# Two-layer hybrid decoder trunk: filter parameters issued later, and adaLN chunks shifted from GpSimd to TensorE

## The chip, the core and the metric

The kernel runs on one core of a Trainium2 chip. The metric is the device time of one execution in microseconds. Three runs of the kernel before took 1825.46, 1830.45 and 1834.98 us; the median is 1830.45 us. The execution that the profiler recorded took 1834.18 us.

## The reference

All data is float32, batch 1, 512 tokens, width 1024, two layers. Cut to what matters here:

```python
cs = silu(c)
for i in range(2):
    mod = cs @ ada_w[i] + ada_b[i]              # 1024 -> 6 * 1024
    sh1, sc1, g1, sh2, sc2, g2 = split(mod, 6)
    h = rms_norm(x, norm_mix_g[i]) * (1 + sc1) + sh1
    mix = hybrid_mixer(h, ...) if i == 0 else conformer_conv(h, ...)
    x = x + g1 * mix
    h = rms_norm(x, norm_ffn_g[i]) * (1 + sc2) + sh2
    x = x + g2 * ((silu(h @ wg) * (h @ wu)) @ wd)
return rms_norm(x, final_norm_g)
```

`hybrid_mixer` runs an SSM (Mamba-2) part and a dilated attention part on one input projection and joins them in one output projection. `conformer_conv` holds a causal depthwise convolution with 31 taps per channel.

## The kernel before

The residual stream lies transposed on the chip: `xT[k]` holds 128 channels by 512 tokens, k from 0 to 7. A matrix product splits weights and activations into a high and a low part (`slab`, lines 196 to 210: one load on the queue SP, a cast on ScalarE in two halves, a subtraction in two halves, `_h` and `_l`) and issues three matmuls per k tile (`products`, lines 212 to 226). Slab buffers come in twos (`wpool`), so a slab's load waits until the subtraction of the slab two before it is done, and its cast until the matmuls of that slab are done.

The stages follow each other: input norm, SSM in four groups (`ssm_inputs` and `ssm_group`), attention in eight pairs of heads with pieces of the output projection between them (`att_pair`, `y_chunk`, `mixed_chunk`), FFN of layer 0, conformer, FFN of layer 1, final norm. The last piece of the output projection, `mixed_chunk(3, ...)`, works in two halves of 256 tokens (names `wa_0_...` and `wa_256_...`), twelve matmuls for each 128 output channels. `residual` (line 608) adds each result to `xT` on VectorE and so frees its bank in PSUM. The norm `n1` before the FFN works in the same halves: `Stat.add` squares on ScalarE (`n_q`) and sums on GpSimd or VectorE (`n_acc`, line 263); `rstd` runs a chain of small VectorE operations (`n_v`, `n_t`, `n_y`); `spread` makes `n_d` on VectorE and `n_b` on TensorE; `finish` makes `n_g`, `n_h` (ScalarE) and `n_l` (VectorE). The first FFN products of both halves (`first_banks`, names `f_a` for gate and `f_b` for up) start with the first `n_h`.

The 6 * 1024 adaLN outputs of a layer are 48 chunks of 128 columns of `ada_w`. For layer 0, chunks 0 to 15 are made on VectorE in the first stage. Chunks 16 to 23 are made on TensorE in the SSM stage (`ada_rows`, after groups 0 and 1, four chunks at a time): eight loads of 128x512 through three buffers, eight matmuls in which `cs32` holds silu(c) in the first of 32 columns, each k going to its own 32 rows of a bank (`adar`), then a copy to SBUF (`adas`) and four small matmuls that sum the rows (`adac`). Chunks 24 to 47 are made on GpSimd in the attention stage, three per pair of heads (`ada_pool`): a load on GpSimd's own queue, a product with silu(c), three additions (`adap`), and a transpose on TensorE (`ada`, line 153) with a sum on VectorE. The chunks of layer 1 are made on VectorE during the FFN of layer 0 (`side`, four chunks per call, `adaa`).

The depthwise convolution of layer 1 needs `taps` (two loads and two transposes, `rows`), `wcol` (one memset and sixteen VectorE copies, line 921) and the filters `w4[0..3]` (four GpSimd products of 128x1024, line 930).

The order of the instructions on each engine is fixed when the program is built: a scheduler in the framework simulates the program and lists each engine's instructions by the time at which they would be ready. `tc.issue_after(x)` makes the instructions of a block on x's engine stand behind x; it holds back no other engine. At run time each engine and each DMA queue takes its instructions in that order.

Of the kernel before, what the change touches and what calls it, by code (L numbers as in the profile page):

```python
# [9 lines left out]
F32 = mybir.dt.float32  # L10
# [3 lines left out]
ALU = mybir.AluOpType  # L14
# [3 lines left out]
P = 128  # L18
# [4 lines left out]
KT = D // P  # L23
# [13 lines left out]
TB = "AABBC"  # L37
XG = 4
NEG = -1e30
LB = (383, 255, 255)  # L40
# [37 lines left out]
def trunk_kernel(ctx: ExitStack, tc, a, out, dbg=None):  # L78
    nc = tc.nc
    V, S, G, PE = nc.vector, nc.scalar, nc.gpsimd, nc.tensor  # L80
# [9 lines left out]
    def bank(tag, name, shape=(P, T)):  # L90
        return psum.tile(list(shape), F32, tag=tag, name=name)
# [52 lines left out]
    adab = [pa[:, 16:64], None]  # L144
# [19 lines left out]

    def ada_rows(pool, l, j0):

        ps = bank("C", f"adar{l}_{j0}")
        for k in range(KT):
            w = pool.tile([P, 512], F32, tag="adaw", name=f"adaw{l}_{j0}_{k}", bufs=3)
            nc.sync.dma_start(w, a["ada_w"][l][k * P:(k + 1) * P, j0 * P:j0 * P + 512])  # L170
            PE.matmul(ps[k % 4 * 32:(k % 4 + 1) * 32, :], cs32[:, k, :], w, start=k < 4, stop=k >= 4)
        rw = tmp.tile([P, 512], F32, tag="st_sq", name=f"adas{l}_{j0}")
        S.copy(rw, ps)
        pm = bank("C", f"adac{l}_{j0}", (P, 4))
        for j in range(4):
            PE.matmul(pm[:, j:j + 1], rw[:, j * P:(j + 1) * P], ones[:, 0:1], start=True, stop=True)
        V.tensor_tensor(mod[l][:, j0:j0 + 4], pm, adab[l][:, j0:j0 + 4], op=ALU.add)

# [377 lines left out]

    jobs = [(0, j) for j in range(24, 48)]

# [19 lines left out]
    for g in range(GROUPS):  # L578
        ssm_group(g, *ins)
        if g < 2:  # L580
            ada_rows(ssm, 0, 16 + 4 * g)
        if g + 1 < GROUPS:
            ins = ssm_inputs(g + 1)
# [250 lines left out]
    nrm = None  # L834
# [75 lines left out]
    dwr = a["cv_w_dw"][0].rearrange("t (k p) -> (t k) p", p=P)  # L910
    taps = const.tile([P, 31 * KT], F32, name="taps")
    rows([(dwr[0:128], 128)], "dw0", taps[:, 0:128])
    rows([(dwr[128:248], 120)], "dw1", taps[:, 128:248])

    wcol = const.tile([P, KT, 4, 8], F32, name="wcol")
    V.memset(wcol[0:32, :, :, 0], 0.0)
    taps3 = taps.rearrange("p (t k) -> p k t", k=KT)
    for sft in range(4):
        for g in range(4):
            o = wcol[sft * 32:(sft + 1) * 32, :, g, 0 if sft else 1:]  # L920
            V.tensor_copy(o, taps3[g * 32:(g + 1) * 32, :, sft - 1 if sft else 3::4])
    id4 = const.tile([P, 32], F32, name="id4")
    nc.sync.dma_start(id4, a["k_cst"][:, C_I4:C_W])
    ctx_d = ExitStack()
    pre = ctx_d.enter_context(tc.tile_pool(name="pre", bufs=1))
    w4 = {}

    def filters(k):
        w4[k] = pre.tile([P, 32, 32], F32, tag="w4", name=f"w4_{k}", bufs=4)
        G.tensor_tensor(w4[k], id4.unsqueeze(1).broadcast_to([P, 32, 32]),  # L930
                        wcol[:, k, :, :].rearrange("p g m -> p (g m)").unsqueeze(2).broadcast_to([P, 32, 32]), op=ALU.mult)

    for k in range(4):
        filters(k)
    nxt = Norm("n2", CUTS)
    with tc.tile_pool(name="ada", bufs=1) as ada:
        wides = [(1, j) for j in range(0, 48, 4)]

        def side():
            for _ in range(2 if len(wides) == 2 else 1):  # L940
                if wides:
                    l, j = wides.pop(0)
                    with tc.issue_after(nrm.tail.ins):
                        ada_wide(ada, "adacc", l, j, ada_load(ada, l, j, G, 2))

        ffn(0, nrm, g_ffn0, nxt, side)
# [185 lines left out]
```

## Time and profile before

| what | value |
|---|---|
| median of three runs | 1830.45 us (1825.46 to 1834.98) |
| profiled execution, its own time | 1834.18 us |
| its span, first to last instruction | 1832.4 us |
| PE / DVE / ACT / POOL busy | 1755.0 / 1006.2 / 740.0 / 356.2 us |
| mean granted TensorE clock | 0.985 |

PE is TensorE, PEld its weight loads, DVE VectorE, ACT ScalarE, POOL GpSimd, SP the queue of the sync engine. Idle time is what the rows put in brackets: how long the engine stood, and the instruction whose end released it. PEclk is the granted clock of TensorE: 1.00 is 2.4 GHz, 0.50 is 1.2 GHz. A row that merges several instructions ends in xN.

### The profile page before, as it was taken

The numbers are of one execution on the slowest core, as the hardware profiler recorded it, in microseconds if no ns is written. First come the engines' busy times: TensorE is split into PE (matmuls) and PEld (weight loads), VectorE is DVE, ScalarE is ACT, GpSimd is POOL, SyncE is SP. The second block draws the span as 40 slices with busy tenths as digits, with TensorE's granted clock in tenths as the row PEclk, the third lists the DMA queues.
The fourth block names the chain that finished last, engine by engine and source line by source line (L and its number), as shares of the span: only waits on it lengthen the run. The fifth ranks groups of instructions, "written<-read, shape, count | busy, mean of one in ns | idle before, by whom it ended". The sixth has DMA issues, their size and how long they took to land.

```text
span 1832.4 us, 25139 instructions
## 1 busy us (share of the span) xinstructions
PE 1755.0 (96%) x9815; PEld 1434.6 (78%) x9815; DVE 1006.2 (55%) x1946; ACT 740.0 (40%) x1475; POOL 356.2 (19%) x286
## 2 busy tenths in 40 slices
PE   5999999999999999887999999999999999999998
PEld 3777677788778787666888888897677988888887
DVE  7756658455655556648765664374216743233336
ACT  6455646455444444334421221254116633132235
POOL 0013314124543433424000000013105100000001
PEclk8999999999999999998999999999999999999999
DMA  9455544445444545334455553243632522223233
GB/s 306 122 146 159 146 124 121 121 135 154 128 138 136 142 121 159 125 104 140 163 194 194 190 196 121 81 156 88 166 103 88 161 92 93 92 92 115 72 96 133
DMA packets 234755, 247.85 MB, mean 135 GB/s; under 512 B 14586, under 2 KB 200764, under 8 KB 234637
## 3 DMA queue, kind: packets, MB, share of 16 engines
q1 hardware_dynamic: 224653, 208.51, 38.1%
q0 software_dynamic: 9984, 37.75, 6.2%
q8 instruction: 77, 1.26, 0.3%
q14 instruction: 41, 0.34, 0.1%
HBM read 228.73 MB, written 8.64 MB: 130 GB/s over the span
## 4 chain that ended last, share of the span: by engine, by line
PE 83%; DVE 6%; DMA 5%; ACT 3%; issue 1%; POOL 1%; SPq 0%; DVEq 0%; ACTq 0%
PE fd L221 4%; PE fd L222 4%; PE fd L224 4%; PE fg L222 4%; PE fg L221 4%; PE fu L222 4%; PE fu L221 4%; PE fu L224 4%; PE fg L224 4%; PE cps L977 3%; PE s L733 2%; DMA ar<-a_dram 2%; PE z L221 2%; PE z L222 2%; PE z L224 2%
## 5 line engine op out<-in xcount | busy, mean ns | idle before, releaser
L221 PE MATMUL fd<-uh,wd_h 128*128 128x512 f32 (+1 forms) x448 | 148.6, 347 | 0.9 <-DVE xT L608 0.9
L209 DVE TENSOR_TENSOR wf_l<-wf_w,wf_h 128x1024 fp32r<-128x1024 f32 x88 | 106.1, 1240 | 75.4 <-ACT wf_h L208 75.4
L222 PE MATMUL fd<-uh,wd_l 128*128 128x512 f32 (+1 forms) x448 | 147.1, 344 | 0.0
L208 ACT CAST wf_h<-wf_w 128x1024 fp32r<-128x1024 f32 x88 | 87.7, 1048 | 116.5 <-PE fd L224 71.9
L263 POOL TENSOR_TENSOR n_acc<-n_acc,n_q 128x256 f32<-128x256 f32 x32 | 29.7, 928 | 525.7 <-ACT n_q L259 525.5
L222 PE MATMUL fg<-n_h,wf_l 128*128 128x512 f32 x320 | 125.3, 392 | 1.0 <-DVE wf_l L209 1.0
L221 PE MATMUL fg<-n_h,wf_h 128*128 128x512 f32 x320 | 125.4, 392 | 0.5 <-ACT wf_h L208 0.5
L222 PE MATMUL fu<-n_h,wf_l 128*128 128x512 f32 x320 | 124.8, 390 | 0.0
L221 PE MATMUL fu<-n_h,wf_h 128*128 128x512 f32 x320 | 124.6, 389 | 0.0
L759 ACT ACTIVATE s<-s,nm 128x128 f32<-128x128 f32 x192 | 79.5, 415 | 47.1 <-DVE nm L755 41.2
L208 ACT CAST wd_h<-wd_w 128x1024 fp32r<-128x1024 f32 (+1 forms) x64 | 57.1, 940 | 101.2 <-PE fd L224 81.1
L885 DVE TENSOR_TENSOR fs<-fs,fu 128x512 f32<-128x512 f32 x40 | 27.5, 688 | 127.3 <-PE fu L224 127.3
L221 PEld LDWEIGHTS fd<-uh,wd_h 128*128 128x128 f32 x448 | 84.1, 188 | 11.9 <-DVE xT L608 1.3
L608 DVE SCALAR_TENSOR_TENSOR xT<-fd,mod,xT 128x512 f32<-128x512 f32 (+1 forms) x64 | 39.0, 615 | 98.4 <-PE fd L224 98.1
L222 PEld LDWEIGHTS fd<-uh,wd_l 128*128 128x128 f32 x448 | 84.2, 188 | 10.5
L224 PE MATMUL fd<-ul,wd_h 128*128 128x512 f32 (+1 forms) x448 | 91.9, 343 | 0.0
L209 DVE TENSOR_TENSOR wd_l<-wd_w,wd_h 128x1024 fp32r<-128x1024 f32 (+1 forms) x64 | 68.2, 1099 | 34.9 <-ACT wd_h L208 34.5
L162 DVE SCALAR_TENSOR_TENSOR adaa<-adaw,cs,adaa 128x512 f32<-128x512 f32 x112 | 84.8, 758 | 2.7
L884 ACT ACTIVATE fs<-fg 128x512 f32<-128x512 f32 x40 | 23.9, 597 | 146.7 <-PE fg L224 146.7
L186 POOL TENSOR_TENSOR adap<-adap 128x512 f32<-128x512 f32 (+2 forms) x72 | 80.9, 1124 | 5.0
L224 PEld LDWEIGHTS fd<-ul,wd_h 128*128 128x128 f32 x448 | 72.9, 188 | 10.6
L224 PE MATMUL fu<-n_l,wf_h 128*128 128x512 f32 x320 | 79.1, 389 | 0.0
(410 smaller groups left out, 4555.8 us busy)
## 6 DMA issues: line engine op xcount, KB each, us to landing
adaw<-in_ada_w POOLq DMA_DIRECT2D x24, 1024.0 KB, 5.6
wf_w<-in_ffn_w_gate SPq DMA_DIRECT2D x22, 1024.0 KB, 5.3
wf_w<-in_ffn_w_up SPq DMA_DIRECT2D x22, 1024.0 KB
wd_w<-in_ffn_w_down SPq DMA_DIRECT2D x16, 1024.0 KB, 5.1
adap<-in_ada_w POOLq DMA_DIRECT2D x24, 512.0 KB, 5.4
wd_w<-in_ffn_w_down SPq DMA_DIRECT2D x16, 768.0 KB, 4.3
wa_w<-in_hy_w_out SPq DMA_DIRECT2D x20, 512.0 KB, 5.7
adaw<-in_ada_w SPq DMA_DIRECT2D x8, 1024.0 KB, 7.8
```

The lines of the kernel that those rows point to most:

```text
L162: V.scalar_tensor_tensor(acc, ws[k // 4][:, k % 4, :], cs[:, k:k + 1], acc, op0=ALU.mult, op1=ALU.add)
L186: G.tensor_tensor(w[:, 0:n], w[:, 0:n], w[:, n:2 * n], op=ALU.add)
L208: S.copy(hi[:, s:e], raw[:, s:e])
L209: eng.tensor_tensor(lo[:, s:e], raw[:, s:e], hi[:, s:e].bitcast(F32), op=ALU.subtract)
L221: PE.matmul(ps[:, cols], hi[:, o(k):o(k) + P], xh, start=k == 0, stop=False)
L222: PE.matmul(ps[:, cols], lo[:, o(k):o(k) + P], xh, start=False, stop=False)
L224: PE.matmul(ps[:, cols], hi[:, o(k):o(k) + P], acts[k][1][:, cols], start=False, stop=k == nk - 1)
L263: (V if k >= self.n - 3 else G).tensor_tensor(self.acc, self.acc, sq, op=ALU.add)
L608: V.scalar_tensor_tensor(xT[m][:, cols], ps[:, cols], mod[l][:, go + m:go + m + 1], xT[m][:, cols], op0=ALU.mult, op1=ALU.add)
L733: marks[hp, 0] = marks[hp, 1] = PE.matmul(ps[:, o:o + 2 * wd].rearrange("p (e w) -> p e w", e=2), q, k, start=True, stop=True)
L759: S.activation(s[:, o:o + wd], s[:, o:o + wd], AF.Exp, bias=nm, accum_out=l)
L977: PE.matmul(ps[g * 32:(g + 1) * 32, :], w4[k][:, g * 8 + m, :], u4[k][:, g, t:t + w], start=m == 0, stop=m == 7)
```

## The change

Three edits. The filter parameters (`taps`, `wcol`, `w4[0..3]`) are issued from the third call of `side` on, in the FFN of layer 0, their VectorE part behind the last instruction of the norm. `ada_rows` takes three chunks at a time: two loads of 128x4x384 through one buffer of their own, each followed by four matmuls of 384 columns, and it is called four times (after group 0 twice, after groups 1 and 2 once). GpSimd makes chunks 28 to 47, twenty in place of twenty-four, three per pair of heads as before, so the last pair has none.

```diff
+ADS = (16, 19), (22,), (25,), ()
...
-    def ada_rows(pool, l, j0):
+    def ada_rows(pool, l, j0, nj):
-        ps = bank("C", f"adar{l}_{j0}")
-        for k in range(KT):
-            w = pool.tile([P, 512], F32, tag="adaw", name=f"adaw{l}_{j0}_{k}", bufs=3)
-            nc.sync.dma_start(w, a["ada_w"][l][k * P:(k + 1) * P, j0 * P:j0 * P + 512])
-            PE.matmul(ps[k % 4 * 32:(k % 4 + 1) * 32, :], cs32[:, k, :], w, start=k < 4, stop=k >= 4)
+        ps, w_ = bank("C", f"adar{l}_{j0}"), nj * P
+        for i in range(2):
+            w = pool.tile([P, 4, 384], F32, tag="adaw", name=f"adaw{l}_{j0}_{i}", bufs=1)[:, :, 0:w_]
+            nc.sync.dma_start(w, a["ada_w"][l][i * 512:(i + 1) * 512, j0 * P:j0 * P + w_].rearrange("(k p) c -> p k c", p=P))
+            for k in range(4):
+                PE.matmul(ps[k * 32:(k + 1) * 32, 0:w_], cs32[:, 4 * i + k, :], w[:, k, :], start=i == 0, stop=i == 1)
...
-    jobs = [(0, j) for j in range(24, 48)]
+    jobs = [(0, j) for j in range(28, 48)]
...
-        if g < 2:
-            ada_rows(ssm, 0, 16 + 4 * g)
+        for j in ADS[g]:
+            ada_rows(ssm, 0, j, 3)
...
+    def conv_params():
+        with tc.issue_after(nrm.tail.ins):
+            rows([(dwr[0:128], 128)], "dw0", taps[:, 0:128])
+            rows([(dwr[128:248], 120)], "dw1", taps[:, 128:248])
+            V.memset(wcol[0:32, :, :, 0], 0.0)
...
+                    V.tensor_copy(o, taps3[g * 32:(g + 1) * 32, :, sft - 1 if sft else 3::4])
+        for k in range(4):
+            filters(k)
...
                 if wides:
+                    if len(wides) == 10:
+                        conv_params()
```

On TensorE the transposes of chunks 46 and 47 (`ada`, line 153) leave the last piece of the output projection, where they stood inside `wa_0_0_...` and between `wa_0_1_2` and `wa_0_1_3`; they now stand a pair of heads earlier.

On VectorE in the second half of that piece (`wa_256_...`, its residual additions at line 608, 610 in the changed program), before the change, the sixteen copies of `wcol` stand ahead of the norm's chain for the first half, which begins with `n_0_v`:

```order
L608 SCALAR_TENSOR_TENSOR xT_218<-wa_256_0_2_0_6983,mod_121,xT_218 128x256
L921 COPY wcol<-taps 32x8x7 x4
L921 COPY wcol<-taps 32x8x8 x12
L278 TENSOR_SCALAR n_0_v<-n_0_s 128x2
L608 SCALAR_TENSOR_TENSOR xT_219<-wa_256_0_3_0_7000,mod_121,xT_219 128x256
L235 TENSOR_SCALAR n_0_t<-n_0_v 128x2
```

In the changed program the chain begins one residual addition earlier:

```order
L211 TENSOR_TENSOR wa_256_1_l<-wa_256_1_w,wa_256_1_h 128x1024
L610 SCALAR_TENSOR_TENSOR xT_217<-wa_256_0_1_0_6940,mod_121,xT_217 128x256
L280 TENSOR_SCALAR n_0_v<-n_0_s 128x2
L237 TENSOR_SCALAR n_0_t<-n_0_v 128x2
L238 TENSOR_SCALAR n_0_y<-n_0_t 128x2
L610 SCALAR_TENSOR_TENSOR xT_218<-wa_256_0_2_0_6957,mod_121,xT_218 128x256
```

The copies now stand among the additions of the third adaLN slab of layer 1, in the FFN.

On VectorE at the end of the same chain, before the change (`n_0_d` feeds the broadcast `n_0_b`, `n_g` is its product, `wf_0_0_l` here is the low part of the first up slab):

```order
L238 TENSOR_TENSOR n_0_t<-n_0_y 128x2
L239 SCALAR_TENSOR_TENSOR n_0_t<-n_0_t,n_0_v 128x2
L608 SCALAR_TENSOR_TENSOR xT_223<-wa_256_1_3_0_7077,mod_121,xT_223 128x256
L240 SCALAR_TENSOR_TENSOR n_0_y<-n_0_t,n_0_y 128x2
L285 TENSOR_SCALAR n_0_d<-cst,n_0_y 128x128 x2
L209 TENSOR_TENSOR wf_0_0_l<-wf_0_0_w,wf_0_0_h 128x1024 x2
L321 TENSOR_TENSOR n_g_0_7206<-n_g_0_7206,n_0_b 128x256
```

In the changed program:

```order
L610 SCALAR_TENSOR_TENSOR xT_221<-wa_256_1_1_0_7017,mod_121,xT_221 128x256
L287 TENSOR_SCALAR n_0_d<-cst,n_0_y 128x128 x2
L610 SCALAR_TENSOR_TENSOR xT_222<-wa_256_1_2_0_7034,mod_121,xT_222 128x256
L265 TENSOR_TENSOR n_256_acc<-n_256_acc,n_256_q_7031 128x256
L265 TENSOR_TENSOR n_256_acc<-n_256_acc,n_256_q_7048 128x256
L610 SCALAR_TENSOR_TENSOR xT_223<-wa_256_1_3_0_7051,mod_121,xT_223 128x256
L323 TENSOR_TENSOR n_g_0_7145<-n_g_0_7145,n_0_b 128x256
```

`n_0_d` stands two residual additions earlier, and the subtraction of the up slab has moved behind the first four `n_g`.

On the queue SP in SSM group 0, before the change (`ar` and `ef` are the group's decay rows, `wz` and `wbc` slabs of the input projection):

```order
L505 DMA ar_0_1449<-a_dram 128x8x128
L170 DMA adaw_16_3_1070<-in_ada_w 128x512
L170 DMA adaw_16_4_1073<-in_ada_w 128x512
L170 DMA adaw_16_5_1076<-in_ada_w 128x512
L505 DMA ar_1_1491<-a_dram 128x8x128
L170 DMA adaw_16_6_1079<-in_ada_w 128x512
L200 DMA wz_1_w<-in_hy_w_in 128x8x256
```

In the changed program:

```order
L507 DMA ar_0_1456<-a_dram 128x8x128
L171 DMA adaw_16_1_1067<-in_ada_w 128x4x384
L507 DMA ar_1_1498<-a_dram 128x8x128
L202 DMA wz_1_w<-in_hy_w_in 128x8x256
L171 DMA adaw_19_0_1081<-in_ada_w 128x4x384
L557 DMA yd_dram<-y_0_846 128x4x512
L202 DMA wbc_w<-in_hy_w_in 128x8x128 x2
L171 DMA adaw_19_1_1087<-in_ada_w 128x4x384
```

Each load of a half slab stands in the queue at its place, behind it the loads of `ar`, `wz`, `wbc` and `wx`.

## Rows read from the trace of the kernel before

**Rows 1.** The page of the profile, its part 1 (busy us, share of the span, instructions per engine) and the engine line of its part 4 (the chain that ended last).

```profile
PE 1755.0 (96%) x9815; PEld 1434.6 (78%) x9815; DVE 1006.2 (55%) x1946; ACT 740.0 (40%) x1475; POOL 356.2 (19%) x286
...
PE 83%; DVE 6%; DMA 5%; ACT 3%; issue 1%; POOL 1%; SPq 0%; DVEq 0%; ACTq 0%
```

**Rows 2.** The waits of TensorE over the whole span: line waited for, total us, times, longest us.

```profile
PE ada L153 <- POOL adap L186: 8.6, 2, 6.1
...
PE n_b L288 <- DVE n_d L285: 4.7, 2, 4.0
...
PE f_a L221 <- ACT n_h L322: 4.1, 2, 3.4
```

**Rows 3.** Stretches between the end of the mixer and the first FFN: length, busy us of PE, PEld, DVE, ACT and POOL with their instruction counts, PEclk (granted TensorE clock as a share of full speed), DMA share, GB/s.

```profile
817.00:821.00 4.00, 3.63 (x15) 3.18 (x16) 1.93 (x5) 0.67 (x3) 0.92 (x1) 0.50 0.50 163
...
821.00:828.40 7.40, 7.40 (x60) 7.06 (x59) 4.29 (x5) 4.61 (x9) 5.78 (x4) 1.00 0.07 23
...
828.40:831.00 2.60, 0.09 (x2) 0.05 (x1) 0.92 (x3) 0.83 (x2) 2.60 (x5) 1.00 0.42 97
...
851.00:856.00 5.00, 1.14 (x6) 1.06 (x6) 4.96 (x5) 2.15 (x3) 5.00 (x3) 0.92 0.36 122
...
861.50:865.00 3.50, 3.44 (x16) 3.44 (x17) 3.50 (x14) 3.50 (x10) 0.00 (x0) 0.50 1.02 404
```

**Rows 4.** TensorE in order of time over the same stretches: start us, us, instruction, and in brackets the idle time before it and what ended it.

```profile
816.95 0.47 PE L153 MATMUL ada<-cst,adap 128*128 128x128 f32 x1 [6.09 <-POOL adap L186]
...
822.32 0.29 PE L221 MATMUL wa<-yh,wa_h 128*128 128x256 f32 x1
...
823.76 0.29 PE L221 MATMUL wa<-yh,wa_h 128*128 128x256 f32 x1
...
830.95 0.33 PE L153 MATMUL ada<-cst,adap 128*128 128x128 f32 x1 [2.51 <-POOL adap L186]
...
861.56 0.58 PE L221 MATMUL f_a<-n_h,wf_h 128*128 128x256 f32 x1 [3.43 <-ACT n_h L322]
...
886.81 0.60 PE L153 MATMUL ada<-cst,adaa 128*128 128x128 f32 x4
```

**Rows 5.** VectorE in order of time over the same stretches, columns as in rows 4.

```profile
809.74 2.35 DVE L209 TENSOR_TENSOR wa_l<-wa_w,wa_h 128x1024 fp32r<-128x1024 f32 x2
...
814.27 1.29 DVE L821 TENSOR_TENSOR at<-o,at 128x512 f32<-128x512 f32 x2 [2.17 <-DMA at<-w_dram]
...
839.29 4.31 DVE L921 COPY wcol<-taps 32x56 f32<-32x56 f32 x16
...
851.35 1.48 DVE L240 SCALAR_TENSOR_TENSOR n_y<-n_t,n_y 128x2 f32<-128x2 f32 x1
...
852.87 3.76 DVE L285 TENSOR_SCALAR n_d<-cst,n_y 128x128 f32<-128x128 f32 x2
...
856.55 4.08 DVE L209 TENSOR_TENSOR wf_l<-wf_w,wf_h 128x1024 fp32r<-128x1024 f32 x2
```

**Rows 6.** GpSimd in order of time (the four filter products), and the row of the tile n_d over the whole span (ns min/median/max).

```profile
850.89 7.53 POOL L930 TENSOR_TENSOR w<-id,wcol 128x1024 f32<-128x1024 f32 x4 [2.23 <-DVE n_t L238]
...
L285 DVE TENSOR_SCALAR n_d<-cst,n_y x12: 280/286/1944, 852.9 to 1459.2; 128x128 f32<-128x128 f32 x12
```

**Rows 7.** ScalarE in order of time, columns as in rows 4.

```profile
816.61 0.62 ACT L826 CAST ath<-at 128x512 fp32r<-128x512 f32 x1 [6.20 <-DVE at L823]
...
850.84 1.99 ACT L208 CAST wf_h<-wf_w 128x1024 fp32r<-128x1024 f32 x2 [0.53 <-PE wa L224]
...
861.00 1.71 ACT L322 ACTIVATE n_h<-n_g,mod 128x256 fp32r<-128x256 f32 x4 [7.85 <-DVE n_g L321]
```

**Rows 8.** The loads of the tile at over the whole span, from issue to landing.

```profile
DMA to landing us min/median/max: 4.0/4.4/6.1
```

**Rows 9.** TensorE in the SSM stage (each pair of a weight load and a matmul counts two in xN), and the transposes of the chunks from GpSimd, ns min/median/max.

```profile
127.91 1.06 PE L171 MATMUL adar<-adaw,cs 128*32 128x512 f32 x6
...
145.41 1.05 PE L171 MATMUL adar<-adaw,cs 128*32 128x512 f32 x2
...
158.09 0.95 PE L176 MATMUL adac<-ones,adas 128*128 128x1 f32 x8
...
L153 PE MATMUL ada<-cst,adap x24: 270/273/475, 420.5 to 831.0; 128*128 128x128 f32 x24
```

**Rows 10.** The queue SP and TensorE in the SSM stage, and two rows of the page's part 6 (KB of one load, median us from issue to landing).

```profile
128.98 1.31 SPq L170 DMA_DIRECT2D adaw<-in_ada_w  x3
...
136.67 1.06 PE L171 MATMUL adar<-adaw,cs 128*32 128x512 f32 x6
...
wd_w<-in_ffn_w_down SPq DMA_DIRECT2D x16, 768.0 KB, 4.3
...
adaw<-in_ada_w SPq DMA_DIRECT2D x8, 1024.0 KB, 7.8
```

**Rows 11.** VectorE in the first FFN's first stretch, and two pieces of the chain that ended last there (start us, us, what).

```profile
914.95 4.68 DVE L162 SCALAR_TENSOR_TENSOR adaa<-adaw,cs,adaa 128x512 f32<-128x512 f32 x6
...
921.18 0.69 DVE L885 TENSOR_TENSOR fs<-fs,fu 128x512 f32<-128x512 f32 x1 [1.55 <-PE fu L224]
...
902.45 1.81 PE fg L224 x8
...
907.89 1.82 PE fu L224 x8
```

More of the change, by code (lines that the diff above doesn't have):

```diff
@@ L163, in ada_wide @@
         return ada_finish(l, acc, j0, 4)
-    def ada_rows(pool, l, j0):
-        ps = bank("C", f"adar{l}_{j0}")
-        for k in range(KT):
-            w = pool.tile([P, 512], F32, tag="adaw", name=f"adaw{l}_{j0}_{k}", bufs=3)
-            nc.sync.dma_start(w, a["ada_w"][l][k * P:(k + 1) * P, j0 * P:j0 * P + 512])
-            PE.matmul(ps[k % 4 * 32:(k % 4 + 1) * 32, :], cs32[:, k, :], w, start=k < 4, stop=k >= 4)
-        rw = tmp.tile([P, 512], F32, tag="st_sq", name=f"adas{l}_{j0}")
-        S.copy(rw, ps)
+    def ada_rows(pool, l, j0, nj):
[5 more added lines that the diff above has]
+                PE.matmul(ps[k * 32:(k + 1) * 32, 0:w_], cs32[:, 4 * i + k, :], w[:, k, :], start=i == 0, stop=i == 1)
+        rw = tmp.tile([P, 512], F32, tag="st_sq", name=f"adas{l}_{j0}")[:, 0:w_]
+        S.copy(rw, ps[:, 0:w_])
         pm = bank("C", f"adac{l}_{j0}", (P, 4))
-        for j in range(4):
+        for j in range(nj):
             PE.matmul(pm[:, j:j + 1], rw[:, j * P:(j + 1) * P], ones[:, 0:1], start=True, stop=True)
-        V.tensor_tensor(mod[l][:, j0:j0 + 4], pm, adab[l][:, j0:j0 + 4], op=ALU.add)
+        V.tensor_tensor(mod[l][:, j0:j0 + nj], pm[:, 0:nj], adab[l][:, j0:j0 + nj], op=ALU.add)
     def ada_pool(pool, bufs, l, j):
@@ L910, in trunk_kernel @@
     dwr = a["cv_w_dw"][0].rearrange("t (k p) -> (t k) p", p=P)
[L911 to L921, printed above, removed]
     id4 = const.tile([P, 32], F32, name="id4")
@@ L926, in trunk_kernel @@
     w4 = {}
+    taps = const.tile([P, 31 * KT], F32, name="taps")
+    wcol = const.tile([P, KT, 4, 8], F32, name="wcol")
+    def conv_params():
[3 more added lines that the diff above has]
+            V.memset(wcol[0:32, :, :, 0], 0.0)
+            taps3 = taps.rearrange("p (t k) -> p k t", k=KT)
+            for sft in range(4):
+                for g in range(4):
+                    o = wcol[sft * 32:(sft + 1) * 32, :, g, 0 if sft else 1:]
+                    V.tensor_copy(o, taps3[g * 32:(g + 1) * 32, :, sft - 1 if sft else 3::4])
+        for k in range(4):
+            filters(k)
     def filters(k):
@@ L931, in filters @@
                         wcol[:, k, :, :].rearrange("p g m -> p (g m)").unsqueeze(2).broadcast_to([P, 32, 32]), op=ALU.mult)
-    for k in range(4):
-        filters(k)
     nxt = Norm("n2", CUTS)
```

## Prediction

> **What bounds the kernel now.** I read the page first: TensorE is busy for 1755.0 of 1832.4 us and makes 83% of the chain that ended last [rows 1]. So the time is TensorE's work plus its idle time and its slow stretches, and an edit pays only where TensorE stands or runs slow. I read TensorE's waits next: the longest wait in the list is for a transpose of adaLN chunks from GpSimd, 8.6 us in two waits, and the norm that follows adds 4.7 us (for n_d) and 4.1 us (for n_h, most of it at the first FFN) [rows 2]. Nearly all of this lies between 810 and 862 us. Then I read that stretch in the windows and in order of time. TensorE is nearly empty from 851 to 861.5 and its granted clock drops after a long idle: 0.50 (1.2 GHz) from 817 to 821 after 6.09 us of idle, 0.50 again from 861.5 to 865 [rows 3, 4]. That is the place that the first edit and the last chunks touch; the rest of the SSM and attention stages is TensorE at work.
>
> **The change part by part.** The sum is made on the profiled execution, 1834.18 us: span 1832.4 and 1.8 around it. It lies 3.7 us above the median of 1830.45, so the saving found here is taken off the median at the end.
>
> The first wait for a chunk, 6.09 us up to 816.95 [rows 4], I cost at nothing. The matmul behind it needs ath, and ScalarE makes ath from 816.61 to 817.23 [rows 7], after VectorE waited for the tile at until 814.27 [rows 5]. So ath takes the place of the chunk. The load of at may land some 1.7 us sooner without the chunk's load beside it (4.4 median against 6.1 at most [rows 8]; I take the most to be this one), but VectorE now does the 2.35 us subtraction, which it did while waiting [rows 5], between the two steps of at. Bounds: 2 us gained, 1 us lost; I take 0.
>
> The second wait, 2.51 us up to 830.95 [rows 4], goes: the matmuls behind it (wa_0_1_3) use the same slab as those ahead of it. TensorE thus goes on at 828.44 with nine pieces of twelve matmuls, one of the first half and eight of the second. A piece takes 1.44 us at full clock (822.32 to 823.76 [rows 4], clock 1.00 [rows 3]), nine take 13.0, so 841.4. VectorE still puts two subtractions (2.35 us [rows 5]) between residual additions that free banks, for which I add 1.6: 843.0.
>
> The norm's chain beside it. Before, the sixteen wcol copies held VectorE for 4.31 us ahead of it, and then the four filter products ran on GpSimd for 7.53 us [rows 5, 6]. While they ran, the two n_d took 3.76 us, and the same operation has a median of 0.286; the two subtractions took 4.08 against 2.35 without them [rows 5, 6]. Those two rows alone lost 3.2 + 1.7 us on the path from the last residual addition to n_g, and n_y beside them took 1.48. All that is gone. In the new order n_d is done before the last piece of the projection ends, so at 843.0 what is left is ScalarE's two casts of the up slab, which wait for that piece's buffer (1.99 [rows 7]) and hide n_b and n_g, then one square, and the first n_h, 0.43 (a quarter of 1.71 [rows 7]); the square has the same size, so I give it 0.43 too. That is 2.9 us. I get the first f_a at 846.0, where it was 861.56 [rows 4]: 15.5 us. The block from f_a to 886.81 [rows 4] keeps its 25.25 us, slow clock included, since a 3 us idle still stands ahead of it. Bounds of this term: 7 (n_h held to 854 by ScalarE or the up slab) and 19 (no late banks, no slow clock).
>
> The Trainium skill bears on the filters (SBUF — State Buffer, "The single rule"): the port pair that VectorE and GpSimd share is an exclusive lock, and the loser waits out the whole instruction. The trace agrees: the longest n_d took 1.94 us, one filter product 1.88 [rows 6]. The rule says that the loss moves with the filters to wherever VectorE has work.
>
> It does move, into the FFN. There VectorE gets 4.31 us of copies, and beside the four filters it loses the 4.9 us seen in the two rows above: 9.2 us, between the additions of the third slab (4.68 us for six [rows 11]) and the next fs, which frees the bank of an up product. Its cover is the 1.55 us for which VectorE waited there [rows 11], and the 5.4 us of the product that comes between (902.45 to 907.89 [rows 11]): 7.0. Left over: 2.2 us of idle TensorE. Below, 0; above, all of 4.31 + 7.53 - 7.0 = 4.8. I take 2. By the lock rule at its worst, four products each waited out in full, it is that upper end.
>
> TensorE in the SSM stage: three adar matmuls of 512 columns span 1.06 us and one alone spans 1.05 [rows 9], so those that go to different rows of the bank run beside each other and the group counts. Before there were two slabs of four groups, 8.4 us; now there are eight groups of four, 384 columns wide: 0.79 us each by columns, 1.4 if the fourth costs a third more, so 6.3 to 11.2; I take the lower half, 7.5, nearest to the rows: 0.9 gained. The adac sums grow from 8 to 12, 0.24 each (0.95 for four [rows 9]): 1.0 lost. Four transposes of 0.27 [rows 9] leave the attention stage: at most 1.1, I take 0.5. Together 0.4 gained, from 3 lost to 3 gained, which also holds what the slightly new order of groups 1 to 3 may shift. The bytes of adaLN weights are the same.
>
> The new buffer: each half slab is loaded only when the four matmuls of the half before are done, and the next loads of SP stand behind it. Before, three loads of 256 KB, the same 768 KB, were issued at 128.98 and used at 136.67 without a wait [rows 10]: 7.7 us of cover, and the new second half stands at the same place. A 768 KB load lands in 4.3 us in one row, a 1024 KB one in 7.8 [rows 10]. I take no wait; bounds 0 and 4 us in all.
>
> Sum: 15.5 - 2 + 0.4 = 13.9, so 1820.3 on the profiled execution and 1816.5 on the median.
>
> **The rivals.** First: the filters cost the FFN more than I think, a backlog that also delays the low parts of the next slabs, 9 us or so (copies and contention uncovered). Gain 15.9 - 9 = 7: 1823.5. For it: the contention seen at the norm. Against: VectorE has idle time in every period there.
>
> Second: n_h stays late. The up slab is loaded by SP only after a subtraction of the projection, cast after its last piece, and ScalarE puts this cast ahead of n_h. If f_a starts at 853 the gain is 8.6 - 1.6 = 7: 1823.5. For it: before, the cast ran at 850.84, as soon as the buffer was free [rows 7]; against: that was before the wait of n_h began.
>
> Third, slower: the single buffer. If each second half lands in 14 us in place of 7.7, because SP stands at an earlier wait or ar loads share the engines, TensorE loses 6 us in each of the four slabs, 25 in all, and the slabs of wx and wz behind come late too: 1841. It decides from a landing of about 13.5 us on. Against it: the 7.8 us of the slowest row like it [rows 10]. The Trainium skill (Trainium Kernel Development and Optimization, "Best Practices") speaks for it: it asks for double buffers so that loads run beside the work. The trace of before shows three buffers and no wait, and no row of it shows one.
>
> Fourth: the change does what it says at the norm, but the wait moves on to the first slabs of the FFN, whose loads now collide with layer 1's adaLN loads on GpSimd's queue: gain 4, 1826.5.
>
> **How the numbers follow.** Forecast 0.66, with its own range of 1810 to 1822; filters in the FFN 0.12; late n_h 0.11; collision of loads 0.06; single buffer 0.05. The measurement can tell about 0.5%, 9.2 us, from no change: faster means below 1821.3. The forecast's upper edge lies just beyond that, so faster gets 0.66 (0.64 of the forecast and 0.02 of the others), within 0.5% gets 0.29, slower 0.05. The range of 1809 to 1827 leaves out the single buffer and the best ends of the terms together.
>
> **What would show it.** Right: no wait of TensorE for GpSimd's chunks; no n_d above 0.3 us before the FFN; some 17.5 us between the end of wa_0_1_2 and the first f_a, in place of 33; a wait of about 2 us in the third FFN period at an up product; adar groups of 0.8 to 1.0 us. Wrong: a wait of TensorE at adar for a load; f_a waiting on ScalarE or on the up slab at 850 or later; an idle TensorE of 5 us or more where the filters now run; a granted clock of 0.5 in the SSM stage.

## The result, and the profile after

| | before | after |
|---|---|---|
| median | 1830.45 us | 1820.54 us (seven runs, 1814.79 to 1822.05) |
| ratio | | 0.9939, 95% interval 0.9922 to 0.9957 |
| profiled execution, its own time | 1834.18 us | 1821.43 us |
| its span | 1832.4 us | 1819.7 us |

The ratio is 11.2 us of 1830.45. The forecast was 1816.5 on the median and 1820.3 on the profiled execution. From here on "the changed kernel" is this one, and its lines stand two below those of before (one in the adaLN helpers).

The page, parts 1 and 4, as in [rows 1]:

```profile
PE 1748.2 (96%) x9851; PEld 1429.8 (79%) x9851; DVE 996.0 (55%) x1940; ACT 740.0 (41%) x1477; POOL 332.3 (18%) x266
...
PE 80%; DMA 6%; DVE 5%; ACT 3%; SPq 2%; issue 2%; POOL 1%; DVEq 0%; ACTq 0%; POOLq 0%
```

TensorE's waits, as in [rows 2] (total us, times, longest):

```profile
PE ada L154 <- DVE adaa L163: 10.1, 4, 6.6
...
PE wa L223 <- ACT ath L828: 5.0, 1, 5.0
PE adar L173 <- DMA adaw<-in_ada_w: 3.4, 1, 3.4
...
PE n_s L272 <- ACT n_q L261: 1.6, 1, 1.6
...
PE ada L154 <- DMA adaw<-in_ada_w: 0.7, 1, 0.7
PE f_a L223 <- ACT n_h L324: 0.6, 1, 0.6
...
PE ada L154 <- POOL adap L188: 0.4, 1, 0.4
```

The 8.6 us for chunks from GpSimd are 0.4, and n_d is no longer waited for. In their place stand ath (the rounded attention output, 5.0) and, new, a half slab in the SSM stage (3.4). TensorE in order of time at the places of [rows 4], at the first products of the second FFN slab pair (`fg` gate, `fu` up), and at its third pair:

```profile
815.68 0.58 PE L223 MATMUL wa<-ath,wa_h 128*128 128x256 f32 x1 [4.99 <-ACT ath L828]
...
844.49 0.61 PE L272 MATMUL n_s<-ones,n_q 128*128 128x1 f32 x4 [1.59 <-ACT n_q L261]
844.96 0.36 PE L223 MATMUL f_a<-n_h,wf_h 128*128 128x256 f32 x1
...
869.64 0.49 PE L223 MATMUL fg<-n_h,wf_h 128*128 128x512 f32 x1 [0.54 <-ACT wf_h L210]
870.87 0.66 PE L154 MATMUL ada<-cst,adaa 128*128 128x128 f32 x4 [0.73 <-DMA adaw<-in_ada_w]
...
912.48 0.44 PE L154 MATMUL ada<-cst,adaa 128*128 128x128 f32 x2 [1.82 <-DVE adaa L163]
913.08 0.50 PE L223 MATMUL fu<-n_h,wf_h 128*128 128x512 f32 x1 [0.16 <-DVE fs L887]
```

The first f_a starts at 844.96 in place of 861.56. The windows, columns as in [rows 3]:

```profile
815.60:819.60 4.00, 3.56 (x15) 3.27 (x16) 1.57 (x3) 0.68 (x3) 0.00 (x0) 0.50 0.71 261
...
845.00:848.00 3.00, 3.00 (x26) 3.00 (x27) 3.00 (x9) 2.35 (x7) 0.00 (x0) 1.00 1.01 396
```

After the wait for ath the granted clock is 0.50, as in [rows 3] after the wait for a chunk; but the first f_a now run at 1.00, where they ran at 0.50. VectorE and GpSimd around the norm and in the FFN, as in [rows 5, 6]:

```profile
840.27 0.54 DVE L287 TENSOR_SCALAR n_d<-cst,n_y 128x128 f32<-128x128 f32 x2
...
900.88 3.80 DVE L931 COPY wcol<-taps 32x56 f32<-32x56 f32 x16
904.71 7.71 DVE L163 SCALAR_TENSOR_TENSOR adaa<-adaw,cs,adaa 128x512 f32<-128x512 f32 x4
```
```profile
904.77 9.44 POOL L937 TENSOR_TENSOR w<-id,wcol 128x1024 f32<-128x1024 f32 x4 [2.76 <-DVE wcol L931]
```

The two n_d take 0.54 us in place of 3.76. The four products now meet VectorE at 904.8: four additions that take 3.1 us by [rows 11] (4.68 for six) take 7.71, and TensorE waits 1.82 + 0.16 us behind them.

### The profile page after: what moved, and what is told of

It reads as the page before. It is cut to its first block, busy times and chain, and to the rows that moved or that the text cites. A ratio compares the mean times of both kernels' runs of the same rounds, so it can differ in the third digit from the quotient of the medians.

```text
span 1819.7 us, 25180 instructions
## 1 busy us (share of the span) xinstructions
PE 1748.2 (96%) x9851; PEld 1429.8 (79%) x9851; DVE 996.0 (55%) x1940; ACT 740.0 (41%) x1477; POOL 332.3 (18%) x266
## 4 chain that ended last, share of the span: by engine, by line
PE 80%; DMA 6%; DVE 5%; ACT 3%; SPq 2%; issue 2%; POOL 1%; DVEq 0%; ACTq 0%; POOLq 0%
PE fd L223 4%; PE fd L224 4%; PE fd L226 4%; PE fu L223 4%; PE fg L224 4%; PE fu L224 4%; PE fu L226 4%; PE fg L226 4%; PE fg L223 4%; PE s L735 2%; SPq L976 2%; DMA ar<-a_dram 2%; PE cps L984 2%; PE z L223 2%; PE z L224 2%
## 5 line engine op out<-in xcount | busy, mean ns | idle before, releaser
L163 DVE SCALAR_TENSOR_TENSOR adaa<-adaw,cs,adaa 128x512 f32<-128x512 f32 x112 | 89.5, 800 | 2.5
L226 PE MATMUL fg<-n_l,wf_h 128*128 128x512 f32 x320 | 79.0, 389 | 0.0
```

Of the source, the lines that this page charges most:

```text
L163: V.scalar_tensor_tensor(acc, ws[k // 4][:, k % 4, :], cs[:, k:k + 1], acc, op0=ALU.mult, op1=ALU.add)
L226: PE.matmul(ps[:, cols], hi[:, o(k):o(k) + P], acts[k][1][:, cols], start=False, stop=k == nk - 1)
```

## The experiments

For every run the start of the same matmul was set against the first profile of before. The table splits the difference (us, less is earlier) at four of them: the start of the last projection piece (808.2 in before), the first f_a (861.6), the first fg (887.2) and the first fd (the down product, 954.4). "End" is the difference at the first fo (the transposes behind the final norm, 1793.0). Each column from "to f_a" to "to fd" is the change within its own stretch; "on the starts" below means read in this way.

| kernel | ratio to before | up to 808 | to f_a | to fg | to fd | end |
|---|---|---|---|---|---|---|
| before_again | one run | -0.9 | +0.1 | +0.1 | 0.0 | -0.8 |
| changed kernel | 0.9939 | -0.1 | -16.5 | -0.9 | +4.2 | -12.7 |
| after_again | 0.9938 | -3.2 | -17.1 | -0.9 | +4.2 | -16.8 |
| filters_only | 0.9962 | +1.6 | -12.1 | +0.2 | +5.2 | -5.2 |
| chunks_only | 0.9986 | -1.7 | -13.3 | +6.4 | +0.9 | -7.7 |
| copies_early | 0.9998 | +1.7 | -14.0 | +8.1 | +0.9 | -3.0 |
| quarters | 0.9953 | +3.4 | -16.4 | -0.9 | +4.1 | -8.0 |
| three_slabs | 0.9924 | 0.0 | -16.6 | -0.9 | +4.2 | -12.9 |
| spread | 0.9905 | -6.9 | -16.5 | -0.9 | +1.7 | -22.1 |
| spread_again | 0.9915 | -1.6 | -16.8 | -0.9 | +1.7 | -17.1 |
| spread_three | 0.9920 | +0.5 | -16.6 | -0.9 | +1.8 | -15.5 |
| spread_skip | 0.9928 | -6.1 | -15.5 | +0.4 | +1.4 | -19.7 |
| four_a_pair | 1.0084 | +26.9 | -15.2 | -1.2 | +5.1 | +16.1 |

Intervals of the ratios are 0.0014 to 0.002 to either side and stand with each run below.

### How far one profile can be trusted

**before_again**, no edit.

> The kernel before, unchanged, for a second profile: how far the start of the same matmul lies from one execution to the next. Theory (the differences of 1 to 5 us between 130 and 780 us from kernel to kernel are mostly of one execution, since the kernel with the filter edit alone has the order of before there and still shows them): differences of 1 to 4 us there against the first profile of before, under 1 us in the stretch from 810 to 960 us taken by itself. Rival (they are the kernels' own): under 1 us everywhere.

The same program differed from itself by 2.4 us at 158 us, 2.8 at 378 and 3.3 at 645, by 0.1 at 778 and 0.9 at 808; from 808 to the first fd by 0.2 in all. The theory holds. **after_again**, no edit:

> The changed kernel once more, beside the next three on the same chip. Theory: 10 to 12 us less than before (ratio 0.9935 to 0.995). Its second profile shows which of the differences up to 800 us belong to the kernel: TensorE's wait for a half slab (3.4 us in the first profile) is there again, the stalls at the first fg (about 1.3 us) and in the third period (2.0 us) are the same within 0.1 us.

1819.59 us, 0.9938 (0.9923 to 0.9953). The half slab was waited for again (3.6 us), the stalls in the FFN were 0.54, 0.72 and 1.82 us; up to 808 it was 3.1 us ahead of the first profile, from 808 to the first fd 0.6. The theory holds. So what follows rests on the last three stretches of the table; of the first one a single profile says little.

### Each edit alone

**filters_only**: in the kernel before, only the filters' edit.

```diff
+    def conv_params():
...
+                    if len(wides) == 10:
+                        conv_params()
```

> The kernel before with the filter edit alone: filter parameters behind the norm, adaLN slabs and the 24 GpSimd chunks as before. Theory (the two edits act one after the other on TensorE, and the filters hold the norm): the waits for chunks stay, about 6 and 2.5 us, the norm is as in the changed kernel; first f_a about 12.5 us earlier than before, the stalls of the first FFN periods (some 1.5 and 2.5 us) appear as in the changed kernel; 9 us less than before, ratio 0.995. Rival A (the chunks decide, the filters only fill a wait that TensorE has anyway): 3 us less or nothing. Rival B (the filter edit is the whole gain, the second chunk wait would be hidden): 11.5 us less or more, first f_a 15 us earlier.

1825.03 us, 0.9962 (0.9945 to 0.9980): 7.0 us less. The waits for chunks were 6.26 and 1.26 us, the first f_a came 12.1 us earlier counted from 808. The theory holds: its 9 us lie inside the interval (3.7 to 10.1 us), both rivals outside. From 808 to the first fd the profile gains 6.7. What is missing has two places, both of the clock. The stall of the third period is the same 1.82 + 0.16 us, but here the granted clock fell behind it, in the changed kernel it did not (fu after the stall, first filters_only, then the changed kernel, columns as in [rows 3]):

```profile
919.60:923.20 3.60, 3.48 (x9) 2.70 (x10) 2.52 (x4) 3.00 (x4) 1.98 (x2) 0.54 0.25 39
```
```profile
913.00:916.60 3.60, 3.52 (x15) 2.92 (x16) 2.52 (x4) 3.01 (x4) 1.94 (x2) 1.00 0.25 39
```

Nine matmuls in 3.6 us against fifteen. And the first f_a ran at 0.61 (851 to 854 us) behind the same wait of 1.59 us behind which they run at 1.00 in the changed kernel; the stretch from f_a to fg is 1.1 us longer (+0.2 against -0.9).

**chunks_only**: the changed kernel with taps, wcol and filters where they stood before.

```diff
+    for k in range(4):
+        filters(k)
...
-                    if len(wides) == 10:
-                        conv_params()
```

> The changed kernel with the filter parameters in their old place: four slabs of three chunks, twenty chunks on GpSimd. The scheduler here puts the sixteen copies into the attention output at the end of the last pair (between at and its low part) and the four filter products behind GpSimd's last sum of the norm. Theory: the copies cost TensorE about 3 us there, the second chunk wait (2.5 us) is gone, n_d is done before the filters begin (no n_d above 0.8 us), but the products meet n_g, n_l and the low part of the up slab, each 1.5 to 2 times as long, some 4 to 5 us ahead of or within the first FFN block; no stall at the third FFN period: 6 us less than before in all (3 to 8). Rival A (only n_d suffers from the filters): 11 us less. Rival B (whatever uses GpSimd beside the norm costs as much as before): 0 to 2 us less.

1827.47 us, 0.9986 (0.9970 to 1.0003): 2.6 us less, and no difference is not excluded. From 808 to the first f_a it gains 13.3 us. Then the four products meet the norm's VectorE work: the low part of the up slab takes 4.12 us in place of 2.35, the first n_l 2.13 in place of 0.48, and TensorE waits 3.44 us for n_h behind them. VectorE, GpSimd and TensorE in order of time:

```profile
845.48 4.12 DVE L211 TENSOR_TENSOR wf_l<-wf_w,wf_h 128x1024 fp32r<-128x1024 f32 x2
849.52 2.13 DVE L325 SCALAR_TENSOR_TENSOR n_l<-n_g,mod,n_h 128x256 fp32r<-128x256 f32 x1
```
```profile
843.75 9.67 POOL L932 TENSOR_TENSOR w<-id,wcol 128x1024 f32<-128x1024 f32 x4 [1.64 <-DVE n_acc L265]
```
```profile
855.53 0.58 PE L223 MATMUL f_a<-n_h,wf_h 128*128 128x256 f32 x1 [3.44 <-ACT n_h L324]
```

From f_a to fg that is 7.3 us more than in the changed kernel (+6.4 against -0.9), where 4 to 5 were expected; the copies cost 1.0 us, not 3. Rival A falls: the two n_d took 0.55 us and the loss came all the same. By the time, the forecast of 6 us lies just outside the interval (-0.5 to 5.5 us) and rival B's 0 to 2 us inside: the place was forecast rightly, the loss there was sized too low.

**copies_early**: copies at their old place in the program, products in the FFN (so it was meant).

```diff
+    rows([(dwr[0:128], 128)], "dw0", taps[:, 0:128])
...
+            V.tensor_copy(o, taps3[g * 32:(g + 1) * 32, :, sft - 1 if sft else 3::4])
...
```

> The changed kernel with the two loads, the transposes and the sixteen copies of the filter parameters back at their old place in the program (the scheduler puts the copies between at and its low part) and only the four filter products in the FFN. Theory (the stall of the third FFN period is the sum of copies and contention): the copies cost about 3 us in the projection, the FFN stall falls from 2.0 to under 0.5 us: 1 us slower than the changed kernel, 11.5 us less than before. Rival (the stall is contention with the products alone): it stays at 1.5 to 2 us, 3 us slower than the changed kernel.

1829.60 us, 0.9998 (0.9984 to 1.0012): the whole gain is gone. The experiment did not do what it was made for. Nothing but the late copies had held the products in the FFN; with the copies early, GpSimd ran them as soon as the first adaLN loads were issued, at 848.15, beside the low part of the up slab. The rows of VectorE, GpSimd and TensorE, and the durations of that operation around it (ns min/median/max):

```profile
848.10 9.78 DVE L211 TENSOR_TENSOR wf_l<-wf_w,wf_h 128x1024 fp32r<-128x1024 f32 x2
```
```profile
848.15 7.51 POOL L936 TENSOR_TENSOR w<-id,wcol 128x1024 f32<-128x1024 f32 x4
```
```profile
856.81 0.80 PE L224 MATMUL f_b<-n_h,wf_l 128*128 128x256 f32 x2 [5.92 <-DVE wf_l L211]
```
```profile
L211 DVE TENSOR_TENSOR wf_l<-wf_w,wf_h x4: 1211/1218/8648, 840.9 to 856.7; 128x1024 fp32r<-128x1024 f32 x4
```

One subtraction of 1.22 us took 8.65: it stood until all four products (7.51) were through. Of the FFN this run shows a third period without copies and without products: there is no stall.

### What the stall in the FFN is made of

**spread**: one product behind the loads of each of four slabs.

```diff
-        for k in range(4):
-            filters(k)
...
+                        ws = ada_load(ada, l, j, G, 2)
+                    if 6 <= len(wides) <= 9:
+                        with tc.issue_after(marks['ada'].ins):
+                            filters(9 - len(wides))
...
```

> The changed kernel with the four filter products apart: the copies where they are, then one product behind the loads of each of four slabs of layer 1, in place of four in a row. Theory (VectorE stands still for as long as a run of GpSimd products lasts: in the changed kernel four additions of the third slab took 7.71 us beside the 9.44 us of products, in place of some 3.1): each product alone costs VectorE at most about 1.9 us, inside the 1.3 to 1.5 us plus 4.9 us for which it waits in every period, so the stall of 2.0 us at the third period's up product falls under 0.5 us: 2 us less than the changed kernel, 13 us less than before. Rival (the copies of 3.8 us make the stall): it stays at 1.5 to 2 us.

1816.69 us, 0.9905 (0.9885 to 0.9925). The copies stand where they stood and TensorE waits nowhere in the period. VectorE, then GpSimd:

```profile
894.07 3.81 DVE L931 COPY wcol<-taps 32x56 f32<-32x56 f32 x16
897.91 4.65 DVE L163 SCALAR_TENSOR_TENSOR adaa<-adaw,cs,adaa 128x512 f32<-128x512 f32 x4
```
```profile
897.96 2.47 POOL L934 TENSOR_TENSOR w<-id,wcol 128x1024 f32<-128x1024 f32 x1 [2.76 <-DVE wcol L931]
...
904.05 1.93 POOL L934 TENSOR_TENSOR w<-id,wcol 128x1024 f32<-128x1024 f32 x1
```

The same four additions take 4.65 us, 3.1 less than beside four products. By the stall the theory holds and the rival falls: the copies alone fit into the cover. The ratio is lower than forecast (17.4 us less than before, forecast 13); 6.9 us of the profile's difference lie ahead of 808. **spread_again**, the same kernel beside the changed one on one chip:

> The kernel with the four filter products apart once more, on the same chip as the changed kernel. Theory (what the spreading gives is the stall of the third period and nothing else): 2 to 3 us less than the changed kernel run beside it, 13 to 14 less than before. Rival (it also shortens the attention stage, as its first profile, 3 us ahead at 748 us where the changed kernel is 4.3 behind, suggests): 6 us less than the changed kernel.

1815.67 us, 0.9915 (0.9900 to 0.9931), where after_again had 0.9938: 3.9 us between the medians, with intervals that overlap. Between fg and fd both profiles are 2.4 us better than both of the changed kernel. The 3 us that the first profile was ahead in the attention stage were not there again (2.9 behind at 748 us), so the theory is nearer. The runs with spread products have the lowest ratios of all (0.9905 to 0.9928, with three_slabs at 0.9924 among them); their intervals overlap.

**spread_skip**: in that kernel, the first call of side makes no slab.

```diff
...
+            calls.append(0)
+            for _ in range(0 if len(calls) == 1 else 2 if len(calls) > 9 else 1):
...
```

> The kernel with spread filter products, and no adaLN slab of layer 1 at the first call of side: the twelve slabs start at the second call, two each in the last two calls. Theory (the 1.3 us that TensorE waits at the first fg, for wf_h and for the first slab's transposes, come from the first slab and its load): these waits go, 1.3 us less than the kernel with spread products. Rival (they come from the first gate and up slabs of the FFN, which land late because the norm ends earlier): the wait for wf_h stays, no change.

1815.80 us, 0.9928 (0.9909 to 0.9946): no gain. The wait for wf_h at the first fg (0.54 us) and the next one (0.73) stayed. But the experiment did not do what it was made for either: the slab of the second call took the place of the first. Its additions begin on VectorE 7.5 us ahead of the first fg in both kernels (first the changed kernel, fg at 869.64, then spread_skip, fg at 865.97):

```profile
862.14 0.48 DVE L161 TENSOR_SCALAR adaa<-adaw,cs 128x512 f32<-128x512 f32 x1
```
```profile
858.46 0.48 DVE L161 TENSOR_SCALAR adaa<-adaw,cs 128x512 f32<-128x512 f32 x1
```

So neither theory nor rival is decided by it. What did change is the clock: behind the wait of 1.59 us ahead of f_a it was granted at 0.50, where spread and the changed kernel have 1.00, and the stretch to fg is 1.3 us longer than there (columns as in [rows 3]):

```profile
840.00:843.20 3.20, 3.20 (x16) 3.20 (x17) 3.20 (x10) 2.55 (x7) 0.00 (x0) 0.50 1.02 396
```

### The slabs in the SSM stage

**quarters**: the same space as two buffers.

```diff
-        for i in range(2):
-            w = pool.tile([P, 4, 384], F32, tag="adaw", name=f"adaw{l}_{j0}_{i}", bufs=1)[:, :, 0:w_]
+        for i in range(4):
+            w = pool.tile([P, 2, 384], F32, tag="adaw", name=f"adaw{l}_{j0}_{i}", bufs=2)[:, :, 0:w_]
...
```

> The changed kernel with each slab of three chunks loaded in four quarters of 128x2x384 through two buffers (the same space as one buffer of 128x4x384). Theory (the wait of 3.4 us of TensorE at the third slab is the single buffer: its second half was issued only when the first half's matmuls were done): a quarter is half as long, so the wait falls to 0 to 2 us and the SSM stage ends 1.5 to 3 us earlier than in the changed kernel. Rival (the load is late because of SP's order and the loads beside it): the wait stays at 3 us or more, no change of time.

1821.35 us, 0.9953 (0.9937 to 0.9969). TensorE's wait for these loads fell from 3.4 us to 0.9, as the theory had it, yet up to 808 us nothing was gained. The rows show why: where the changed kernel waits for the half slab, TensorE now waits for `sx`, work of ScalarE on an SSM input, and before it waited there for `sc`, such work on VectorE (first before, then quarters):

```profile
216.65 0.57 PE L221 MATMUL x<-n_h,wx_h 128*128 128x512 f32 x1 [2.45 <-DVE sc L460]
```
```profile
220.28 0.77 PE L223 MATMUL x<-n_h,wx_h 128*128 128x512 f32 x1 [3.85 <-ACT sx L459]
```

**three_slabs**: chunks 16 to 27 in the old form.

```diff
-ADS = (16, 19), (22,), (25,), ()
+ADS = (16,), (20,), (24,), ()
...
```

> The changed kernel with the old form of the adaLN slabs in the SSM stage, three of four chunks (chunks 16 to 27, after groups 0, 1 and 2), each of eight loads of 128x512 through three buffers; the same twenty chunks on GpSimd. Theory (the slabs of three chunks through one buffer cost the SSM stage 2 to 4 us: by the medians so far the kernels with them lose that much against what the end of the mixer and the FFN gain): no wait of TensorE for these loads, SSM stage 2 to 4 us shorter than in the changed kernel: 13 to 15 us less than before. Rival (the number of slabs or the moved order costs it, not the form): same time as the changed kernel within 1.5 us.

1821.17 us, 0.9924 (0.9907 to 0.9941), 2.7 us under the changed kernel by the ratio, with intervals that overlap. TensorE's wait for a load was 0.4 us in all (adar, whole span); for sc it stood 2.85 us at the same place, and at 808 the profile was where that of the changed kernel was. Neither theory nor rival is excluded by the time. **spread_three**: this form with spread products.

> The kernel with spread filter products and the three slabs of four chunks through three buffers. Theory (the wait for a half slab is taken up by later waits of the attention stage, so the form of the slabs is worth nothing at the end): within 1.5 us of the kernel with spread products run beside it. Rival (it costs its 3.4 us): 3 us less.

1815.13 us, 0.9920 (0.9904 to 0.9935), 0.5 us from spread_again: the theory holds. This wait of 3 us in the SSM stage does not show at the end within what the runs can tell.

### GpSimd free at the end, by another way

**four_a_pair**: filters_only with the 24 chunks in the first six pairs.

```diff
-        ada_some(att, 1, 3)
+        ada_some(att, 1, 4)
```

> The kernel before with the filter edit, and its 24 chunks on GpSimd made four per pair of heads in the first six pairs (in place of three in each of eight); slabs in the SSM stage as before. Theory (what the chunk edit gives at the end of the mixer comes from GpSimd's being free in the last pair, not from the twelve chunks on TensorE): no wait for a chunk there, the SSM stage as before, first f_a as in the changed kernel; 13 us less than before, against some 7 for the filter edit alone. Rival (a fourth chunk per pair overloads GpSimd, whose chunks then hold the transposes of the pairs 0 to 5): waits of TensorE for chunks of 5 us or more in the attention stage, 7 us less than before or fewer.

1849.72 us, 1.0084 (1.0066 to 1.0102), the only kernel slower than before. The end of the mixer came as hoped (15.2 us gained from 808 to f_a), but 26.9 us were lost ahead of it. Not for chunks: TensorE's waits for these are 2.4 us in all. In the changed order at stands ahead of score work on VectorE and waits for its load, and the scores of TensorE stand behind it, 5.47 us here and 6.1 once more; these two are 11.5 of the 26.9 us, the rest was not taken apart. So the theory on the end of the mixer holds, and the way to it costs more than it gives. VectorE, then TensorE:

```profile
481.58 1.29 DVE L821 TENSOR_TENSOR at<-o,at 128x512 f32<-128x512 f32 x2 [5.47 <-DMA at<-w_dram]
```
```profile
482.32 2.08 PE L733 MATMUL s<-kz,q 128*128 128x256 f32 x4 [5.47 <-DVE at L821]
```

## Why the prediction was right, step by step

The forecast of 1816.5 lay 4.0 us under the median, and 1820.3 lay 1.1 us under the profiled execution. The gain is where it was expected, at the norm, and there the forecast holds to 0.3 us. That the whole sum lands so near the profile is in part luck: 1.1 us at the first wait and 0.9 from f_a to the first fg were gained beyond it, 2.2 between fg and fd lost beyond it, and up to 808 us two profiles of the same changed kernel lie 3.1 us apart.

**The first wait costs nothing**: right. ath took the chunk's place, 4.99 us for 6.09, and in every run with the chunk edit it stood there with 4.6 to 5.0. The 1.1 us gained lie inside the bounds. As worked out, at came sooner (VectorE takes it at 810.82 in place of 814.27) and the subtraction of 2.35 us stands between its two steps. The 6.1 us that the prediction took for this load belongs to another one, issued at 566.34; the landing of this one is not in the trace.

**The second wait, the pieces and the norm, 15.5 us**: right. From the matmul behind the first wait to the first f_a the forecast had 29.05 us (816.95 to 846.0), the profile has 29.28 (815.68 to 844.96), before it was 44.61 [rows 4]. The projection's last matmul ended at 842.09, where 843.0 was forecast; the matmuls of n_b and n_s follow to 842.90, then the wait of 1.59. What the prediction did not name is the clock's part: before, the granted clock was 0.50 from 831.3 to 834.7, behind the second wait, and from 844.9 to 848.3; in the changed kernel it is 1.00 from 819.8 on. The pieces were costed at full clock, and so the sum has this gain in it. The causes have been separated: without the filters' edit the norm's stretch loses 7.3 to 9.0 us from f_a to fg (chunks_only, copies_early), without the chunk edit 4.4 less is gained up to f_a (filters_only). Neither edit gives the result alone: 7.0 and 2.6 us, 11.2 together.

**The block of f_a keeps its length, slow clock included**: wrong, by 1.1 us (24.14, from 844.96 to 869.10, in place of 25.25). TensorE stood 1.59 us ahead of it, not 3, and the granted clock stayed at 1.00. The one does not settle the other: behind the same 1.59 us the clock was low in filters_only, chunks_only, copies_early and spread_skip (0.61, 0.68, 0.50 and 0.50 in the first 3 us of f_a). With 0.54 us of idle at its end the start of fg came 0.9 us nearer to f_a.

**The filters in the FFN, 2 us, bounds 0 and 4.8**: right in place and size. The period's stall is 1.82 + 0.16 us at an up product, 2.5 us on the starts. Four products in a row are its cause, since four apart do away with it while the copies stay. The working had copies and contention as one sum of 9.2 us; here they are 3.80 and 4.6 (7.71 less 3.1), 8.4.

**What was not in the sum**: 1.3 us of idle at the first fg (0.54 and 0.73). It is in every kernel that has both edits in full; the other four with one of them or a part have 1.0 us there, for wf_l. The fourth rival spoke of a wait at this place, at 9.9 us (13.9 less the 4 it left) and for loads. The rows show another cause. The four casts of wf_h stand on ScalarE right behind the second `fs<-f_a`, which needs the last matmul of f_a; the loads of wf_w had been issued 28 and 22 us earlier (839.98 and 846.28), and others of them land in 8.5 us at most. Before, 19 matmuls of f_b came behind that last f_a (884.53 to 886.97) and covered the first cast; now 10 do (867.75 to 869.10). ScalarE before, then in the changed kernel:

```profile
884.73 0.60 ACT L884 ACTIVATE fs<-f_a 128x512 f32<-128x512 f32 x1 [0.51 <-PE f_a L224]
885.23 3.88 ACT L208 CAST wf_h<-wf_w 128x1024 fp32r<-128x1024 f32 x4
```
```profile
868.06 0.59 ACT L886 ACTIVATE fs<-f_a 128x512 f32<-128x512 f32 x1
868.55 3.88 ACT L210 CAST wf_h<-wf_w 128x1024 fp32r<-128x1024 f32 x4
```

The 0.73 us are the last addition of the first adaLN slab: VectorE makes it from 870.07 to 870.82, the transposes start at 870.87. The view names a load there, but in the other profiles with this wait it names the addition. On the starts the stretch to fd lost 4.2 in place of 2; 0.7 of this are transposes that stood ahead of fg before and now stand behind it.

**The SSM stage, 0.4 gained, bounds 3 to either side, and 0 to 4 for the buffer**: the parts are as worked out, the sum is open. An adar group takes 0.85 us (0.94 was taken), three adac sums 0.72 to 0.83. The second half of the third slab was issued when the first half's matmuls (210.41) were done, and landed 10.2 us later, where 7.8 was the slowest row like it; loads of wz (1 MB) and ar (0.5 MB) had been issued 1.1 and 0.6 us ahead of it. SP, TensorE, and the page's part 6:

```profile
211.72 1.49 SPq L171 DMA_DIRECT2D adaw<-in_ada_w  x1
```
```profile
221.94 1.02 PE L173 MATMUL adar<-adaw,cs 128*32 128x384 f32 x8 [3.36 <-DMA adaw<-in_ada_w]
```
```profile
adaw<-in_ada_w SPq DMA_DIRECT2D x8, 768.0 KB, 10.2
```

So the third rival's mechanism was there once, short of the 13.5 us from which it decides, and no wait was the wrong value to take. The Trainium skill's "Best Practices" (Trainium Kernel Development and Optimization) ask for double buffers; the trace agrees in so far as two smaller buffers cut the wait to 0.9 us, and the runs add that the time did not follow, since another wait stood at the same place (2.45 us before, 3.85 in quarters). By the ratio the changed kernel gains 11.2 us, from 808 on its profiles show 12.6 to 13.6; the 2 us between could be this stage, but two profiles have it at -0.1 and -3.2 up to 808, and no run here settles it. All profiles together say a little more. At the first matmul of the attention output (o, 399.6 in before) the ten with the chunk edit stand 2.2 to 7.6 us behind the first profile of before, 5.0 on average; the four without it 0 to 3.1, 1.9 on average. So the SSM stage seems to have lost some 3 us in place of gaining 0.4, three_slabs and spread_three (5.8 and 5.0) no less than the others, and by 808 this is made up. Why is open.

**The other rivals**: filters at 9 us in the FFN did not come, though beside the norm they do cost 7 to 9. n_h was not late: f_a at 844.96, not 853.

**The signs**: the signs of being right came, if not all to the letter: 0.4 us of waits for GpSimd's chunks, n_d at 0.35 us at most, 18.0 us between the end of wa_0_1_2 (826.98) and the first f_a. Of the signs of being wrong two came all the same: the wait at adar (3.4 us), and a granted clock of 0.50 in the SSM stage (140.6 to 144.0, 222.5 to 225.9 and 297.6 to 301.0). The second was a poor sign, since it is in before too (216.9 to 220.3).

## What to carry to other kernels

Look at what runs on GpSimd beside a chain on which TensorE waits, and move it as single instructions, each into a period in which VectorE has slack; four in a row cost TensorE 2.5 us in the FFN and 7 to 9 beside the norm, four apart in the FFN nothing that shows. Before a wait is taken away, look at what stands behind it: here the wait for a load only hid another of about the same length. When two things hold the same stretch, take each away alone as well as both: here each by itself gave 2.6 and 7.0 us, both 11.2, which the intervals do not tell from the sum. Before a difference of a few microseconds between two profiles is explained, profile the same program twice and use only the stretches in which it agrees with itself.

## What was not expected of the hardware

One VectorE subtraction was shut out for four GpSimd products in a row (8.65 us, usually 1.22, copies_early). In the changed kernel the two took turns: no addition took over 2.29 us (ns min/median/max of the tile), and the four products took 9.44 us in place of 7.51. It is not the operation that decides: in chunks_only the same two subtractions met the same products and took turns, 1.26 and 2.93 us. Nor is every operation held: four n_g, with one input in PSUM, took 0.41 us each there while the first product ran (843.75 to 845.66), as they do without it.

```profile
L163 DVE SCALAR_TENSOR_TENSOR adaa<-adaw,cs,adaa x112: 740/752/2290, 7.6 to 1095.6; 128x512 f32<-128x512 f32 x112
```

The Trainium skill (SBUF — State Buffer, "Who interferes with whom", the single rule) has an exclusive lock for the whole instruction. The turns agree with it (one addition of 0.75 us took 2.29, one product takes 1.88); the 8.65 us do not fit one instruction waited out, but four. What decides between the two cases was not tried.

The same stall of 2.0 us was followed by a granted clock of 0.54 for 3.6 us in filters_only and of 1.00 in the changed kernel. Other profiles fit: four_a_pair, the other kernel with this stall and without the chunk edit, has 0.53 there, and after_again, quarters and three_slabs have 1.00. The wait of 1.59 us ahead of f_a likewise was followed by 0.50 in spread_skip and 0.61 in filters_only, and by 1.00 in the changed kernel. The price of a wait of this size is thus not its length alone: the stall cost 2.5 us in the changed kernel and 4.1 in filters_only on the starts (there -9.2 to -5.1 between the last fg ahead of it and the first fg behind it). What decides is open.
